# A hybrid attention and recurrence block: paired v products, the recurrence's products spread over four array tiles, and four changes of order

## The chip, the cores and the metric

The kernel is one program on one core of a Trainium2 chip. The core has five engines that work side by side, each through its own list of instructions in order: PE (the matrix engine, with its weight loads shown as PEld), DVE (the vector engine), ACT (the scalar engine), POOL and SP; SP and POOL mainly issue DMA transfers here. An instruction that needs a result of another engine waits at a semaphore, and all that stands behind it in its engine's list waits too. Results of PE land in PSUM, which is divided into banks of 128 partitions x 512 fp32 values; DVE and ACT read them from there ("evacuate" them) into SBUF.

The metric is the device time of one execution in microseconds (us). The kernel before takes 1640.1 us, the median of three runs that lie between 1639.86 and 1641.15 us.

## The reference

One block of a hybrid network works on 1024 positions of width 1024. Its input is normed and modulated, projected by one wide matrix, and goes through attention with a forget gate (8 heads) and through a recurrence (8 heads of width 64), whose outputs are gated, merged and projected; a feed-forward part with a convolution of width 3 follows.

```python
h = x
u = modulate(rms_norm(h, ln1_g), shift1, scale1)
q, k, v, f, p_rwkv, p_gate = split(u @ w_in)
o_fox = fox_attention(q, k, v, log_sigmoid(f + fox_b_f))
o_rwkv = rwkv7_time_mix(p_rwkv, ...)
merged = gate_fox * (o_fox @ fox_w_out) + gate_rwkv * (o_rwkv @ rwkv_w_out)
h = h + gate1 * (merged @ w_o)
h = h + gate2 * conv_ffn(modulate(rms_norm(h, ln2_g), shift2, scale2))
return rms_norm(h, final_g)

# the recurrence of one head inside rwkv7_time_mix, position by position
sa    = state @ a_t                                   # a_t = -kk
state = state * w_t + outer(sa, kk * a) + outer(v_t, k_t)
y_t   = state @ r_t
# then y is normed per head (mean, variance), a bonus is added, and it is multiplied by a gate
```

## The kernel before, in words

The part that matters here is the recurrence stage, from about 160 to 600 us of the span. It does three kinds of work at once, and a planner (`Weave`, in the code) interleaves them:

- **The recurrence in chunks.** The 8 heads are four head pairs p, and the 1024 positions two halves hf; that makes 8 units, k = 0 to 7 in the order (0,0), (0,1), (1,0) ... (3,1). A unit has 8 chunks of 64 positions. In place of a scan over positions, each chunk is solved with matrix products and one triangular inverse. `pre(k, p, hf)` prepares a unit (elementwise work, the products `p`, `q`, and the inverse), `main(k, p, hf)` finishes it.
- **Projections for attention and the recurrence**: `rkv_items` and `qk_steps` (products `ps_rkv`, `qk`), `gate_steps` (products `gt`).
- **The v projection of attention**, `v_steps`: 2 groups j of heads, each with 8 tiles t of 128 positions, 24 matmuls per tile (product `v`). ACT copies the result rounded (`vs`, L984) and DVE writes the remainder (`vs`, L985), and a DMA writes both to memory. Each tile has a PSUM tile of its own from the pool `big`, of which it uses 256 of 512 columns.

The order in which PE works is written by the planner and held as it is written. The order on the other engines is set by a scheduler when the kernel is built; it goes by its own estimates of when each operand is ready, and a few manual rules ("not before that one") bind it.

Inside a unit the steps are these. The matrices `E` are made from the products `p` (L794). The corner blocks of 32 x 32 of all chunks are inverted by 62 DVE steps, pairs of L814 (`t`) and L816 (`E`); their operands travel by DMA, `E` to `sm` to `M`, and the result by DMA, `E` to `se` to `TT`. Behind that `main` makes the other corners of the inverse: DVE transposes a corner (`X`, L872), PE makes the products `xi` and `zi`, ACT copies both out. Then the inverse products `uw`: for each of the 8 chunks and each of 2 heads one matmul of 64 rows by 64 columns with 128 values streamed, 16 in all. Chunks 0 to 3 go into one PSUM bank and 4 to 7 into another; head 0 uses rows and columns 0 to 63 of the array, head 1 uses 64 to 127. DVE copies one half of each result out (`Wt`, L900), ACT the other (`UV`, L902). The products `mz`, `sp`, `yp` and a chain of states `S` follow. At the end DVE subtracts the mean in `y` (L953): `mu` is the per-head mean of y, `va` that of its square, both made by `head_sums`, which also uses ACT (`Ztr`, `Zts`) and POOL (`Wtr`, `Wts`, L722).

Some further names: `QA` are operands of `uw`, copied by DVE at L841 and, from the product `q`, at L853; `ql` (L423) is the evacuation of a product `qk` on DVE; `k`, `v`, `r` of L397 are the evacuations of `ps_rkv`; `al` and `bk` at L772 to L774 are elementwise operands of `pre`.

Of the kernel before, what the change touches and what calls it, by code (L numbers as in the profile page):

```python
# [12 lines left out]
ALU = mybir.AluOpType  # L13
# [3 lines left out]
S = 1024  # L17
KT = 8
NH = 512
# [3 lines left out]
CH = 64  # L23
NCU = NH // CH
# [11 lines left out]
NOSYNC = mybir.DependencyInfo(mybir.DependencyClass.NoSync, mybir.DependencyReason.DATA)  # L36
# [98 lines left out]
def hybrid_block(ctx: ExitStack, tc: tile.TileContext, a, out):  # L135
    nc = tc.nc
    weave = Weave()
    ctx.enter_context(tc.manual_schedule(engines={mybir.EngineType.PE}))

    def mm(o, lhsT, rhs, start, stop, more=False):  # L140

        weave.mm_cost(o, lhsT, rhs)
        nc.tensor.matmul(o, lhsT, rhs, start=start, stop=stop, skip_group_check=more)  # L143
# [5 lines left out]
    def f32(ap):  # L149
        return ap.bitcast(F32)  # L150

    tt, stt, ts = nc.vector.tensor_tensor, nc.vector.scalar_tensor_tensor, nc.vector.tensor_scalar
# [15 lines left out]
    def V(name, i=0, n=1):  # L168
        o, _ = VEC[name]
        return vec[:, o + i : o + i + n]  # L170
# [78 lines left out]

    marks = {}  # L250
    held = []

    def behind(i, x):
        if x in marks:
# [119 lines left out]
    with ExitStack() as es:  # L374
# [4 lines left out]
        def big(name):  # L379
            return pb.tile([128, NH], F32, tag="big", name=name)  # L380

        def gen(name):
            return pr.tile([128, NH], F32, tag="gen", name=name)

        def shifted(w, ti, hf, dst, prev, name, by_kt=False):

            ps = big(f"ps_{name}{hf}")
            yield from gemm_steps(ps, w, u, slice(hf * NH, hf * NH + NH), by_kt=by_kt)
            sh = shp.tile([128, NH + 1], F32, tag="sh", name=f"sh_{name}{hf}")
            if hf == 0:  # L390
                nc.vector.memset(sh[:, 0:1], 0.0)
            else:
                nc.vector.tensor_copy(sh[:, 0:1], prev)
            nc.scalar.activation(sh[:, 1 : NH + 1], ps, AF.Copy, scale=V("mu", ti))
            if hf == 0:
                nc.gpsimd.tensor_copy(prev, sh[:, NH : NH + 1])
            marks["bank"] = stt(dst, ps, omu[:, ti : ti + 1], sh[:, 0:NH], op0=ALU.mult, op1=ALU.add)  # L397

        rkv, got, last_col = {}, {}, {}

# [13 lines left out]
        def qk_steps(w, i):  # L414
            sc_ = 0.125 if i < 4 else 1.0
            for hf in range(2):
                cs = slice(hf * NH, hf * NH + NH)
                ps = big(f"qk{i}_{hf}")
                yield from gemm_steps(ps, w, u, cs)
                hi = gsp.tile([128, NH], F32R, tag="sp0", name=f"qh{i}_{hf}")  # L420
                nc.scalar.activation(hi, ps, AF.Copy, scale=sc_)
                lo = gsp.tile([128, NH], F32R, tag="sp0", name=f"ql{i}_{hf}")
                stt(lo, ps, sc_, f32(hi), op0=ALU.mult, op1=ALU.subtract)  # L423
                h0 = 2 * (i % 4)
                for t, k, r0 in ((hi, 0, 0), (lo, 0, 64), (hi, 2, 0)) if i < 4 else ((hi, 1, 0), (hi, 1, 64), (lo, 3, 0)):
                    for h in range(2):
                        nc.sync.dma_start(f32(d_st[h0 + h, k, r0 : r0 + 64, cs]), f32(t[h * 64 : h * 64 + 64, :]))
# [274 lines left out]
        def c3(ap):  # L702
            return ap.rearrange("p (c s) -> p c s", s=CH)
# [23 lines left out]
        def pre(k, p, hf):  # L727
# [41 lines left out]
            tt(bk[:, :, 0, :], c3(kr), c3(en), op=ALU.mult)  # L769
            nc.gpsimd.tensor_copy(bk[64:128, :, 2, :], bk[64:128, :, 0, :])  # L770
            tt(ar[:, 1], c3(rr), el[:, :, 1:], op=ALU.mult)
            ts(al, al, V("k_a", p), oka[:, p : p + 1], op0=ALU.mult, op1=ALU.add)  # L772
            tt(al, al, kk, op=ALU.mult)
            tt(bk[:, :, 1, :], c3(al), c3(en), op=ALU.mult)  # L774
            pcd = chunk_tile("pcd", 3, NCU)
            nc.gpsimd.tensor_copy(pcd, el[:, :, CH])
            rkb = tmp("ksq")
# [33 lines left out]
            for s in range(31):  # L811
                J, W = s // 4 + 1, 31 - s
                tv = t32[:, 0 : J * W].rearrange("p (j w) -> p j w", w=W)
                tt(tv, E32[:, 0:J, s : s + 1].to_broadcast([128, J, W]),  # L814
                   M32[:, s : s + 1, s + 1 : 32].to_broadcast([128, J, W]), op=ALU.mult)
                tt(E32[:, 0:J, s + 1 : 32], E32[:, 0:J, s + 1 : 32], tv, op=ALU.add)  # L816
            se = scr.tile([2, NCU, 2, 32, 32], F32, tag="se", name=f"se{n}")
            for g in range(4):
# [31 lines left out]
            for c in range(NCU):  # L850
                for h in range(2):
                    mm(q[HS[h], c * CH : c * CH + CH], E[HS[1 - h], c, h, 0, :], UV[HS[1 - h], c, h, :], start=True, stop=True)
            nc.vector.tensor_copy(QA[:, :, 0, :], c3(q))  # L853
            bp = gen(f"bs{n}")
            yield from head_sums(bp, rkb, tmp("kr", dt=F32R), tmp("al", dt=F32R), True)
            bon = tmp("bon", bufs=2)
# [3 lines left out]
        def main(k, p, hf):  # L860
# [9 lines left out]
            yield max(0, o["ready"] - weave.now - 2500)  # L870
            for h in range(2):
                i = nc.vector.transpose(X[B0[h], :, :], TT[B0[h], :, 0:32])  # L872
                for x in ("S", "E", "bank") if k == 0 else ("S", "E", "QA") if k > 4 else ("S", "E"):
                    if x in marks:
                        tc.add_manual_dep(i.ins, marks[x].ins.name, NOSYNC)
            yield max(1300, o["ready"] - weave.now)
# [13 lines left out]

            yield 2000
            Wt = rw.tile([128, NCU, CH], F32, tag="Wt", name=f"Wt{n}", bufs=1)
            for c0 in range(0, NCU, 4):
                ps = gen(f"uw{n}{c0}")
                for c in range(c0, c0 + 4):
                    for h in range(2):
                        x = (c - c0) * 128
                        mm(ps[HS[h], x : x + 128], TT[HS[h], c, :], QA[HS[h], c, :, :], start=True, stop=True)
                pv = ps.rearrange("p (c a s) -> p c a s", a=2, s=CH)
                nc.vector.tensor_copy(Wt[:, c0 : c0 + 4, :], pv[:, :, 1, :])  # L900
                for h in range(2):
                    nc.scalar.copy(UV[HS[h], c0 : c0 + 4, h, :], pv[HS[h], :, 0, :])  # L902
            yield 2970
            Zt = rw.tile([128, NCU, CH], F32, tag="Zt", name=f"Zt{n}", bufs=1)
            for c0 in range(0, NCU, 4):
# [44 lines left out]
            mu = gen(f"mu{n}")  # L950
            yield 700
            yield from head_sums(mu, y, part("Zt", "r"), part("Wt", "r"))
            stt(y, mu, -1.0 / CH, y, op0=ALU.mult, op1=ALU.add)  # L953
            ysq = rw.tile([128, NH], F32, tag="ysq", name=f"ysq{n}", bufs=1)
            nc.scalar.activation(ysq, y, AF.Square)
            yield 2700
# [13 lines left out]
        def v_steps(w, j):  # L970

            for t in range(8):
                ts_ = slice(t * 128, t * 128 + 128)
                ps = big(f"v{j}_{t}")
                n = 0
                for wi, xi in ((0, 0), (0, 1), (1, 0)):
                    for kt in range(KT):
                        c0 = (kt % 4) * 256
                        mm(ps[:, 0:256], u[xi][:, kt, ts_], w[kt // 4][wi][:, c0 : c0 + 256], start=n == 0, stop=n == 23)
                        n += 1  # L980
                        yield
                vs = gsp.tile([128, 4, 2, 64], F32R, tag="sp0", name=f"vs{j}_{t}")
                pv = ps[:, 0:256].rearrange("p (h d) -> p h d", d=64)
                nc.scalar.copy(vs[:, :, 0, :], pv)  # L984
                tt(vs[:, :, 1, :], pv, f32(vs[:, :, 0, :]), op=ALU.subtract)  # L985
                nc.sync.dma_start(f32(d_v[4 * j : 4 * j + 4, :, t, :]).rearrange("h p x -> p h x"), f32(vs).rearrange("p h a d -> p h (a d)"))
# [1111 lines left out]
```

## Time and profile before

| | |
|---|---|
| median of 3 runs | 1640.1 us |
| profiled execution, its own time | 1639.56 us |
| its span (first to last instruction) | 1637.8 us |
| PE busy | 1600.6 us, 98% |
| DVE busy | 1214.5 us, 74% |
| ACT busy | 827.8 us, 51% |
| POOL busy | 157.4 us, 10% |
| mean granted clock of PE | 0.996 |

The profile shows one execution. Its chain of waits is the list of work that ended last, followed back from the end; shares are of the span. A group of rows gives engine, operation, tile and shape, with its count and the duration of one (minimum, median and maximum in ns, or the mean). In a timeline each row has its start (us from the start of the span), its length, engine, line, operation, output and input, shape and count, and in brackets the idle time of the engine just before it and who ended it. The ends of matmuls are modelled, so their rows overlap a little; their starts are measured.

### The profile page before, as it was taken

The numbers are of one execution on the slowest core, as the hardware profiler recorded it, in microseconds if no ns is written. First come the engines' busy times: TensorE is split into PE (matmuls) and PEld (weight loads), VectorE is DVE, ScalarE is ACT, GpSimd is POOL, SyncE is SP. The second block draws the span as 40 slices with busy tenths as digits, with TensorE's granted clock in tenths as the row PEclk, the third lists the DMA queues.
The fourth block names the chain that finished last, engine by engine and source line by source line (L and its number), as shares of the span: only waits on it lengthen the run. The fifth ranks groups of instructions, "written<-read, shape, count | busy, mean of one in ns | idle before, by whom it ended". The sixth has DMA issues, their size and how long they took to land.

```text
span 1637.8 us, 25963 instructions
## 1 busy us (share of the span) xinstructions
PE 1600.6 (98%) x9678; PEld 1334.4 (81%) x9678; DVE 1214.5 (74%) x2343; ACT 827.8 (51%) x1557; POOL 157.4 (10%) x189
## 2 busy tenths in 40 slices
PE   8999999999999999999999999999999999999998
PEld 7777787888978788888878888888888888888886
DVE  5786787878876536888679548987777777886677
ACT  5563344444455656778623225644444444555455
POOL 0011101111111011333122000000000000000000
PEclk9999999999999999999999999999999999999999
DMA  9496645543333336434197521232332332675363
GB/s 341 128 328 204 177 130 143 141 114 92 115 104 96 97 121 165 128 103 121 44 357 264 187 81 39 71 135 97 114 105 97 101 105 96 232 249 161 122 212 109
DMA packets 123542, 238.79 MB, mean 146 GB/s; under 512 B 42188, under 2 KB 51284, under 8 KB 123416
## 3 DMA queue, kind: packets, MB, share of 16 engines
q1 hardware_dynamic: 114936, 218.77, 41.2%
q0 software_dynamic: 8480, 18.37, 4.2%
q8 instruction: 76, 1.25, 0.3%
q14 instruction: 50, 0.41, 0.1%
HBM read 172.57 MB, written 64.50 MB: 145 GB/s over the span
## 4 chain that ended last, share of the span: by engine, by line
PE 71%; DVE 6%; ACT 2%; issue 1%; DMA 1%; SPq 1%; POOL 0%; DVEq 0%; POOLq 0%; ACTq 0%
PE X L143 15%; PE D L143 13%; PE Y L143 7%; PE gt L143 6%; PE wo L143 5%; PE br L143 4%; PE rk_ps L143 4%; PE W L143 4%; PE ps_rkv L143 3%; PE ov L143 2%; PE lg L143 2%; PE tp L147 1%; PE v L143 1%; PE sp L143 1%; DVE quads L1082 1%
## 5 line engine op out<-in xcount | busy, mean ns | idle before, releaser
L143 PE MATMUL D<-op,op 128*128 128x512 f32 x924 | 209.8, 389 | 0.0
L143 PEld LDWEIGHTS D<-op,op 128*128 128x128 f32 x924 | 173.3, 188 | 36.3 <-DVE op L1302 0.3
L143 PE MATMUL X<-T_m,S 128*128 128x512 f32 x440 | 107.1, 390 | 0.0
L143 PEld LDWEIGHTS X<-T_m,S 128*128 128x128 f32 x440 | 82.4, 188 | 17.8 <-ACT T_m L1781 0.5
L1301 ACT CAST op<-g 128x512 fp32r<-128x512 f32 x77 | 47.8, 621 | 73.0 <-PE D L143 48.2
L1302 DVE TENSOR_TENSOR op<-g,op 128x512 fp32r<-128x512 f32 x77 | 53.0, 689 | 40.8 <-ACT op L1301 40.8
L1560 DVE SCALAR_TENSOR_TENSOR c<-ab,vec,c 128x512 f32<-128x512 f32 x88 | 65.8, 750 | 18.4 <-ACT c L1563 16.8
L814 DVE TENSOR_TENSOR t<-E,M 128x60 f32<-128x60 f32 (+24 forms) x248 | 56.4, 227 | 27.5 <-DMA M<-sm 21.5
L1526 DVE TENSOR_TENSOR A<-ur,A 128x512 fp32r<-128x512 f32 x64 | 44.0, 689 | 38.3 <-ACT A L1522 38.2
L1526 DVE TENSOR_TENSOR S<-ur,S 128x512 fp32r<-128x512 f32 x66 | 45.5, 691 | 35.2 <-ACT S L1522 35.1
L1522 ACT CAST S<-ur 128x512 fp32r<-128x512 f32 x66 | 41.0, 622 | 57.3 <-DVE ur L1515 30.3
L298 DVE TENSOR_TENSOR lo_in<-raw_in,hi_in 128x512 fp32r<-128x512 f32 x84 | 57.6, 726 | 15.8 <-PE gt L143 4.8
L143 PE MATMUL Y<-T_h,A 128*128 128x512 f32 x264 | 63.4, 389 | 0.0
L143 PE MATMUL Y<-T_h,S 128*128 128x512 f32 x264 | 63.3, 389 | 0.0
L1122 DVE TENSOR_TENSOR tl<-tp,th 128x512 fp32r<-128x512 f32 (+1 forms) x80 | 50.0, 631 | 15.3 <-ACT th L1119 14.9
L1522 ACT CAST A<-ur 128x512 fp32r<-128x512 f32 x64 | 39.6, 621 | 42.9 <-PE X L143 33.4
L296 ACT CAST hi_in<-raw_in 128x1024 fp32r<-128x1024 f32 x42 | 43.8, 1048 | 34.2 <-PE qk L143 14.0
L816 DVE TENSOR_TENSOR E<-E,t 128x60 f32<-128x60 f32 (+24 forms) x248 | 56.0, 226 | 6.3
L143 PE MATMUL W<-B_f,A 128*128 128x512 f32 x252 | 60.6, 389 | 0.0
L143 PE MATMUL X<-B_b,A 128*128 128x512 f32 x252 | 60.5, 389 | 0.0
L143 PEld LDWEIGHTS Y<-T_h,S 128*128 128x128 f32 x264 | 49.6, 188 | 10.3
L143 PEld LDWEIGHTS Y<-T_h,A 128*128 128x128 f32 x264 | 49.5, 188 | 10.3
(491 smaller groups left out, 4143.1 us busy)
## 6 DMA issues: line engine op xcount, KB each, us to landing
raw_in<-in_w_in SPq DMA_DIRECT2D x50, 512.0 KB
wm<-in_w_mod SPq DMA_DIRECT2D x48, 512.0 KB
ur<-in_w_up SPq DMA_DIRECT2D x44, 512.0 KB
g<-d_g SPq DMA_DIRECT2D x35, 512.0 KB
d_g<-gs SPq DMA_DIRECT2D x44, 256.0 KB
d_g<-c SPq DMA_DIRECT2D x33, 256.0 KB
d_st<-qh SPq DMA_DIRECT2D x64, 128.0 KB
stA<-d_st POOLq DMA_DIRECT2D x8, 1024.0 KB, 7.3
```

What stands on the lines that cost most here:

```text
L143: nc.tensor.matmul(o, lhsT, rhs, start=start, stop=stop, skip_group_check=more)
L147: nc.tensor.transpose(o, i, eye)
L296: nc.scalar.copy(hi, raw)
L298: nc.vector.tensor_tensor(lo[:, c : c + NH], raw[:, c : c + NH], f32(hi[:, c : c + NH]), op=ALU.subtract)
L814: tt(tv, E32[:, 0:J, s : s + 1].to_broadcast([128, J, W]), M32[:, s : s + 1, s + 1 : 32].to_broadcast([128, J, W]), op=ALU.mult)
L816: tt(E32[:, 0:J, s + 1 : 32], E32[:, 0:J, s + 1 : 32], tv, op=ALU.add)
L1122: tt(tl[:, 0:w], tp[:, 0:w], f32(th[:, 0:w]), op=ALU.subtract)
L1301: nc.scalar.copy(hi, src)
L1302: tt(lo, src, f32(hi), op=ALU.subtract)
L1522: nc.scalar.copy(hi, src)
L1526: tt(lo, src, f32(hi), op=ALU.subtract)
L1560: stt(c, ab[:, x + hf * NH : x + hf * NH + NH], V("conv_w", 22 * x + i), c, op0=ALU.mult, op1=ALU.add)
```

## The change

It has five parts.

1. **Paired v products.** A tile `v` of odd t no longer takes a PSUM tile of its own. It writes columns 256 to 511 of the bank in whose columns 0 to 255 the even tile before it stands.
2. **Steps behind read-outs.** The three `al` operations of a unit (L772 to L774) are remembered, and if an evacuation on DVE (L397 or L423) is written within 3000 ns of the planner's time after them, they are bound to come behind it on DVE (`evac_done`).
3. **The first step behind the copy.** The first step of the first unit's inverse is bound to come behind the copy of `q` into `QA` (`after_this`).
4. **The odd chunks' products in the other half.** In `uw`, even chunks keep their places in the array and go to one bank; odd chunks take the other half of the columns (head 0 rows 0 to 63 and columns 64 to 127, head 1 the reverse) and go to a second bank. The two kinds alternate. The copies `Wt` become one of 128 x 256 and two of 64 x 256 instead of two of 128 x 256; those of `UV` stay four.
5. **Transpositions behind y.** For k above 4, the transposes `X` (L872) are bound to come behind the last `y` (L953).

```diff
+    soft = []
+    def evac_done(i):
+        for x, t in soft:
+            if weave.now - t < 3000:
+                tc.add_manual_dep(x.ins, i.ins.name, NOSYNC)
+        soft.clear()
+        return i
+    first_step = []
+    def after_this(i):
+        for x in first_step:
+            tc.add_manual_dep(x.ins, i.ins.name, NOSYNC)
...
-            marks["bank"] = stt(dst, ps, omu[:, ti : ti + 1], sh[:, 0:NH], op0=ALU.mult, op1=ALU.add)
+            marks["bank"] = evac_done(stt(dst, ps, omu[:, ti : ti + 1], sh[:, 0:NH], op0=ALU.mult, op1=ALU.add))
...
-                stt(lo, ps, sc_, f32(hi), op0=ALU.mult, op1=ALU.subtract)
+                evac_done(stt(lo, ps, sc_, f32(hi), op0=ALU.mult, op1=ALU.subtract))
...
-            ts(al, al, V("k_a", p), oka[:, p : p + 1], op0=ALU.mult, op1=ALU.add)
-            tt(al, al, kk, op=ALU.mult)
-            tt(bk[:, :, 1, :], c3(al), c3(en), op=ALU.mult)
+            soft.clear()
+            soft.append((ts(al, al, V("k_a", p), oka[:, p : p + 1], op0=ALU.mult, op1=ALU.add), weave.now))
+            soft.append((tt(al, al, kk, op=ALU.mult), weave.now))
+            soft.append((tt(bk[:, :, 1, :], c3(al), c3(en), op=ALU.mult), weave.now))
...
+                if k == 0 and s == 0:
+                    first_step.append(i)
...
-            nc.vector.tensor_copy(QA[:, :, 0, :], c3(q))
+            after_this(nc.vector.tensor_copy(QA[:, :, 0, :], c3(q)))
+            first_step.clear()
...
-                for x in ("S", "E", "bank") if k == 0 else ("S", "E", "QA") if k > 4 else ("S", "E"):
+                for x in ("S", "E", "bank") if k == 0 else ("S", "E", "QA", "y") if k > 4 else ("S", "E"):
...
-            for c0 in range(0, NCU, 4):
-                ps = gen(f"uw{n}{c0}")
-                for c in range(c0, c0 + 4):
-                    for h in range(2):
-                        x = (c - c0) * 128
-                        mm(ps[HS[h], x : x + 128], TT[HS[h], c, :], QA[HS[h], c, :, :], start=True, stop=True)
-                pv = ps.rearrange("p (c a s) -> p c a s", a=2, s=CH)
-                nc.vector.tensor_copy(Wt[:, c0 : c0 + 4, :], pv[:, :, 1, :])
+            ps = [gen(f"uw{n}{e}") for e in range(2)]
+            for c in range(NCU):
                 for h in range(2):
-                    nc.scalar.copy(UV[HS[h], c0 : c0 + 4, h, :], pv[HS[h], :, 0, :])
+                    x = c // 2 * 128
+                    mm(ps[c % 2][HS[h ^ c % 2], x : x + 128], TT[HS[h], c, :], QA[HS[h], c, :, :], start=True, stop=True)
+            pv = [x.rearrange("p (c a s) -> p c a s", a=2, s=CH) for x in ps]
+            nc.vector.tensor_copy(Wt[:, 0::2, :], pv[0][:, :, 1, :])
+            for h in range(2):
+                nc.vector.tensor_copy(Wt[HS[h], 1::2, :], pv[1][HS[1 - h], :, 1, :])
+            for e in range(2):
+                for h in range(2):
+                    nc.scalar.copy(UV[HS[h], e::2, h, :], pv[e][HS[h ^ e], :, 0, :])
...
-            stt(y, mu, -1.0 / CH, y, op0=ALU.mult, op1=ALU.add)
+            marks["y"] = stt(y, mu, -1.0 / CH, y, op0=ALU.mult, op1=ALU.add)
...
-                ps = big(f"v{j}_{t}")
+                if t % 2 == 0:
+                    pair = big(f"v{j}_{t}")
+                ps = pair[:, t % 2 * 256 : t % 2 * 256 + 256]
...
-                        mm(ps[:, 0:256], u[xi][:, kt, ts_], w[kt // 4][wi][:, c0 : c0 + 256], start=n == 0, stop=n == 23)
+                        mm(ps, u[xi][:, kt, ts_], w[kt // 4][wi][:, c0 : c0 + 256], start=n == 0, stop=n == 23)
...
-                pv = ps[:, 0:256].rearrange("p (h d) -> p h d", d=64)
+                pv = ps.rearrange("p (h d) -> p h d", d=64)
```

What this does to the engines' lists shows at three places. On PE the sequence of work is the same in both, apart from the inner order of `uw`. The first place is PE where tile 5 of the second group of v products begins (`v1_4` is tile 4 of group 1; `hi_v`, `lo_v` are the two parts of the weights, and "waits DVE" means a wait at DVE's semaphore). Before:

```order
L143 MATMUL v1_4_4900<-lo_v10_4418,u_hi_107 128x256 x4
L143 MATMUL v1_4_4900<-lo_v11_4425,u_hi_107 128x256 x4
L143 MATMUL v1_5_5001<-hi_v10_4417,u_hi_107 128x256 [waits DVE_49]
L143 MATMUL v1_5_5001<-hi_v10_4417,u_hi_107 128x256 x3
L143 MATMUL v1_5_5001<-hi_v11_4424,u_hi_107 128x256 x4
```

and with the change, on the same engine at the same place:

```order
L143 MATMUL v1_4_4899<-lo_v10_4418,u_hi_107 128x256 x4
L143 MATMUL v1_4_4899<-lo_v11_4425,u_hi_107 128x256 x4
L143 MATMUL v1_4_4899<-hi_v10_4417,u_hi_107 128x256 [waits DVE_49]
L143 MATMUL v1_4_4899<-hi_v10_4417,u_hi_107 128x256 x3
L143 MATMUL v1_4_4899<-hi_v11_4424,u_hi_107 128x256 x4
```

Both begin the new tile with a wait for DVE. Before, the value waited for was that of the remainder `vs` of the tile two before (`v1_3`), whose PSUM tile `v1_5` takes over; now it is that of the tile just before, `v1_4`, because both lie in one bank and the framework counts a bank as one object. The same holds for all eight odd tiles.

The second place is DVE around the remainder of that tile 4. Before, the steps of the inverse stand at a width of 14 there (the last number of `128x5x14`; it falls by one with each pair of steps):

```order
L814 TENSOR_TENSOR t322_1_4562<-E322_1_4560,M322_1_4555 128x70
L773 TENSOR_TENSOR al3_0_4808<-al3_0_4808,k30_4094 128x512
L816 TENSOR_TENSOR E322_1_4560<-E322_1_4560,t322_1_4562 128x5x14
L985 TENSOR_TENSOR vs1_4_4997<-v1_4_4900,vs1_4_4997 128x4x64
L774 TENSOR_TENSOR bk3_0_4888<-al3_0_4808,en3_0_4815 128x8x64
L778 SCALAR_TENSOR_TENSOR ksq3_0_4973<-r30_4093,vec_72,al3_0_4808 128x512
L814 TENSOR_TENSOR t322_1_4562<-E322_1_4560,M322_1_4555 128x65
```

and with the change:

```order
L828 TENSOR_TENSOR t322_1_4562<-E322_1_4560,M322_1_4555 128x42
L787 TENSOR_TENSOR al3_0_4807<-al3_0_4807,k30_4093 128x512
L832 TENSOR_TENSOR E322_1_4560<-E322_1_4560,t322_1_4562 128x7x6
L1006 TENSOR_TENSOR vs1_4_4996<-v1_4_4899,vs1_4_4996 128x4x64
L788 TENSOR_TENSOR bk3_0_4887<-al3_0_4807,en3_0_4814 128x8x64
L792 SCALAR_TENSOR_TENSOR ksq3_0_4972<-r30_4092,vec_72,al3_0_4807 128x512
L828 TENSOR_TENSOR t322_1_4562<-E322_1_4560,M322_1_4555 128x35
```

The remainder stands between the same neighbours, but the inverse has gone on from a width of 14 to one of 6: eight pairs of steps, 16 instructions, stand ahead of it now that stood behind it. The remainder of tile 2 of the same group comes 7 steps later in the same way, and that of tile 4 of the first group 5 steps later.

The third place is DVE where `y` of unit 4 (`y2_0`) meets the transposes `X2_1` of unit 5. Before:

```order
L841 COPY QA3_0_5099<-at3_0_5270 64x4x64 x4
L872 STREAM_TRANSPOSE X2_1_5383<-TT2_1_4630 32x256
L953 SCALAR_TENSOR_TENSOR y2_0_5152<-mu2_0_5154,y2_0_5152 128x512
L872 STREAM_TRANSPOSE X2_1_5383<-TT2_1_4630 32x256
L853 COPY QA3_0_5099<-q3_0_5320 128x8x64
L814 TENSOR_TENSOR t323_0_5194<-E323_0_5192,M323_0_5187 128x31
```

and with the change:

```order
L857 COPY QA3_0_5096<-at3_0_5267 64x4x64 x4
L972 SCALAR_TENSOR_TENSOR y2_0_5149<-mu2_0_5151,y2_0_5149 128x512
L889 STREAM_TRANSPOSE X2_1_5380<-TT2_1_4630 32x256 x2
L828 TENSOR_TENSOR t323_0_5191<-E323_0_5189,M323_0_5184 128x31
L832 TENSOR_TENSOR E323_0_5189<-E323_0_5189,t323_0_5191 128x31
```

The subtraction now stands ahead of both transposes. In SP's list at that point, the DMAs `se2_1` and `TT2_1`, which feed these transposes, move ahead of the last writes of `vs`; before they stood behind them, and `TT2_1` in the middle of the four DMAs `sm3_0` that feed the next unit's inverse.

More of the change, by code (lines that the diff above doesn't have):

```diff
@@ L813, in pre @@
                 tv = t32[:, 0 : J * W].rearrange("p (j w) -> p j w", w=W)
-                tt(tv, E32[:, 0:J, s : s + 1].to_broadcast([128, J, W]),
-                   M32[:, s : s + 1, s + 1 : 32].to_broadcast([128, J, W]), op=ALU.mult)
+                i = tt(tv, E32[:, 0:J, s : s + 1].to_broadcast([128, J, W]),
+                       M32[:, s : s + 1, s + 1 : 32].to_broadcast([128, J, W]), op=ALU.mult)
+                if k == 0 and s == 0:
+                    first_step.append(i)
                 tt(E32[:, 0:J, s + 1 : 32], E32[:, 0:J, s + 1 : 32], tv, op=ALU.add)
```

## The prediction

> **What bounds the kernel now.** I read the page's busy times first, then the chain of waits by engine, then the clock.
>
> ```profile
> PE 1600.6 (98%) x9678; PEld 1334.4 (81%) x9678; DVE 1214.5 (74%) x2343; ACT 827.8 (51%) x1557; POOL 157.4 (10%) x189
> PE 71%; DVE 6%; ACT 2%; issue 1%; DMA 1%; SPq 1%; POOL 0%; DVEq 0%; POOLq 0%; ACTq 0%
> core 0: 1637.8 us, clock 0.996
> ```
>
> The reader sees one engine that is busy for 98% of the span and granted its full clock. So time falls only where PE's own work shrinks or where it stands still, and every new wait of PE costs its length. The waits of PE between 160 and 610 us, the recurrence stage, are few (total us, times, longest):
>
> ```profile
> PE qk L143 <- DVE ql L423: 2.3, 1, 2.3
> PE ps_rkv L143 <- DVE k L397: 1.4, 1, 1.4
> PE v L143 <- DVE vs L985: 1.3, 2, 0.8
> PE sp L143 <- ACT S L933: 0.9, 1, 0.9
> PE va L143 <- POOL Wts L722: 0.9, 1, 0.9
> PE mu L143 <- POOL Wtr L722: 0.7, 1, 0.7
> PE va L143 <- ACT Zts L719: 0.6, 1, 0.6
> PE zi L143 <- ACT X L882: 0.6, 1, 0.6
> ```
>
> They add to 8.7 us: that is all that moving steps can win here. Two stretches matter for what follows, since the v products lie in them (length; busy us and instructions of PE, PEld, DVE, ACT, POOL; PE's clock; DMA share; GB/s):
>
> ```profile
> 314.20:346.00 31.80, 31.33 (x373) 29.03 (x370) 30.15 (x96) 13.23 (x29) 4.51 (x8) 1.00 0.34 106
> 417.50:446.00 28.50, 27.72 (x336) 26.21 (x335) 26.60 (x87) 10.55 (x24) 2.07 (x6) 1.00 0.29 85
> ```
>
> DVE is busy for 95% and 93% there. A result that PE wants from DVE comes late in these stretches, whenever PE asks.
>
> **Part 1, paired v products.** The work stays the same; what changes is which remainder `vs` an odd tile waits for. In the rows of before, each odd tile's start on PE and the remainder of the even tile just ahead stand as follows, tiles 1, 5, 7 of the first group and 1, 3, 5, 7 of the second:
>
> ```profile
> 323.03 0.77 PE L143 MATMUL v<-hi_v,u_hi 128*128 128x256 f32 x5
> 324.46 0.42 DVE L985 TENSOR_TENSOR vs<-v,vs 128x256 fp32r<-128x256 f32 x1
> 342.85 0.86 PE L143 MATMUL v<-hi_v,u_hi 128*128 128x256 f32 x5 [0.47 <-DVE vs L985]
> 343.79 0.42 DVE L985 TENSOR_TENSOR vs<-v,vs 128x256 fp32r<-128x256 f32 x1
> 351.09 0.28 PE L143 MATMUL v<-hi_v,u_hi 128*128 128x256 f32 x1
> 351.70 0.42 DVE L985 TENSOR_TENSOR vs<-v,vs 128x256 fp32r<-128x256 f32 x1
> 411.83 0.40 PE L143 MATMUL v<-hi_v,u_hi 128*128 128x256 f32 x2
> 413.62 0.42 DVE L985 TENSOR_TENSOR vs<-v,vs 128x256 fp32r<-128x256 f32 x1
> 421.83 0.40 PE L143 MATMUL v<-hi_v,u_hi 128*128 128x256 f32 x2
> 424.00 0.42 DVE L985 TENSOR_TENSOR vs<-v,vs 128x256 fp32r<-128x256 f32 x1
> 434.20 0.52 PE L143 MATMUL v<-hi_v,u_hi 128*128 128x256 f32 x3
> 437.78 0.42 DVE L985 TENSOR_TENSOR vs<-v,vs 128x256 fp32r<-128x256 f32 x1
> 441.68 0.40 PE L143 MATMUL v<-hi_v,u_hi 128*128 128x256 f32 x2
> 442.76 0.42 DVE L985 TENSOR_TENSOR vs<-v,vs 128x256 fp32r<-128x256 f32 x1
> ```
>
> The wait now needed is the remainder's start plus 0.42 less PE's start: 1.85, 1.36, 1.03, 2.21, 2.59, 4.00 and 1.50 us, 14.5 us in all. Tile 3 of the first group has other work of PE between it and tile 2, and costs nothing. PE's list keeps its order, so nothing can be done in these waits: behind the waiting matmul stand the rest of the tile, then the recurrence's products.
>
> The sum of lags isn't yet the answer, for two reasons. While PE waits, DVE works on at its own pace, so inside one dense stretch the later lags contain the earlier waits. And the order on DVE moves: the remainders of tile 4 (first group), tile 2 and tile 4 (second group) come 5, 7 and 16 steps later. A step costs what this group says (busy us, mean ns of one, then idle before):
>
> ```profile
> L814 DVE TENSOR_TENSOR t<-E,M 128x60 f32<-128x60 f32 (+24 forms) x248 | 56.4, 227 | 27.5 <-DMA M<-sm 21.5
> ```
>
> 5, 7 and 16 times 0.227 are 1.1, 1.6 and 3.6 us. First stretch: PE is 1.85 late after tile 1, and 1.36 + 1.1 = 2.5 late after tile 5 (the larger, not the sum); tile 7 lies behind the stretch and adds its 1.0: 3.5 us. Second stretch: 2.2 after tile 1, 2.6 + 1.6 = 4.2 after tile 3, 4.0 + 3.6 + 0.4 = 8.0 after tile 5 (the 0.4 is one more copy `Wt`, part 4); there the old wait of tile 6 for that same remainder, 0.8, falls away, and tile 7 adds 1.5: 8.7 us. Part 1 costs **12.2 us**. Its bounds: the shortest lag of a row, 1.03, seven times is 7.2 (DVE free whenever asked); all lags and all moves added up is 14.5 + 6.3 = 20.8.
>
> **Part 4, `uw` over four tiles of the array.** In the chain of waits, the first and last of four units in which PE paces itself (us, length):
>
> ```profile
> 374.75 1.89 PE uw L143 x32
> 570.24 1.89 PE uw L143 x32
> L143 PE MATMUL uw<-QA,TT x256: 269/269/320, 230.3 to 571.9; 64*64 64x128 f32 x128
> 465.29 0.69 PE L143 MATMUL xi<-X,E 32*32 32x32 f32 x32
> L900 DVE COPY Wt<-uw x16: 415/418/425, 234.0 to 572.2; 128x256 f32<-128x256 f32 x16
> ```
>
> 32 records in 1.89 us, of which the last takes 0.27, start (1.89 - 0.27)/31 = 52 ns apart, though each lasts 269: two halves of the array overlap already. The `xi` row has starts 16 ns apart with shorter operands, so issuing isn't the limit. If four quarters overlap as well as two, a unit's starts need half of 1.7 us and it saves 0.85; if not, nothing. No row shows four quarters at once. I take 0.85, because the overlap that the rows do show is one without loss. Only four units (1_1, 2_1, 3_0, 3_1) lie where PE isn't soon stopped by DVE or POOL; in the others PE arrives earlier at a wait that doesn't move. That is **-3.4 us**, between 0 and -6.8 (all eight). The price is one more copy on DVE per unit, at most 0.42 us, hidden where DVE has slack and counted above where it hasn't. The four `UV` copies on ACT, busy half of the time, stay four.
>
> The Trainium skill, "TensorEngine Tiling (Array Packing)", section "Available Configurations" and "Key Properties", lists 64 x 64 as four tiles that run independently; by it the saving is the 0.85 I take, and the sum without that would stand 3.4 us higher. This case's trace shows only two of them at work.
>
> **Parts 2 and 3, the first copy and the steps behind read-outs.**
>
> ```profile
> 179.77 0.19 DVE L814 TENSOR_TENSOR t<-E,M 128x31 f32<-128x31 f32 x1 [7.01 <-DMA M<-sm]
> 180.11 0.68 DVE L853 COPY QA<-q 128x512 f32<-128x512 f32 x1
> ```
>
> DVE sat idle for 7 us while the 0.68 us copy stood behind a step that waited for a DMA. Now it runs in that hole, and `ql`, for which PE waits 2.3 us, comes 0.7 to 1.0 earlier; `k`, for which it waits 1.4, gets `al` (0.5) out of its way. I take -1.4 together and give 0.3 back at the wait of `mu` for POOL, which keeps its own pace: **-1.1 us**, between 0 and -3.7 (both waits gone).
>
> **Part 5, transpositions behind y.**
>
> ```profile
> 458.40 0.43 DVE L872 STREAM_TRANSPOSE X<-TT 32x256 f32<-32x256 f32 x1 [3.23 <-DMA TT<-se]
> 458.86 0.69 DVE L953 SCALAR_TENSOR_TENSOR y<-mu,y 128x512 f32<-128x512 f32 x1
> 461.56 2.77 DMA M<-sm
> ```
>
> DVE stood 3.23 us at a transpose whose operand was on its way, with `y` behind it, and the waits of `va` (0.9 and 0.6) and of `zi` (0.6) follow. With `y` ahead, and `TT` asked for earlier on SP, all three should go: **-2.1 us**, between 0 and -2.1. What can be late next is the transpose; its operand's DMAs stand ahead of the last writes of `vs` now, so I see no cost.
>
> **The sum.** 12.2 - 3.4 - 1.1 - 2.1 = +5.6 us. Behind the recurrence PE is again the bound, and the shift stays whole. The profiled execution took 1639.56 us and becomes 1645.2; the median of the runs lies 0.5 above it, so I predict 1645.7 us. 0.2% (3.3 us) is about what a measurement of this kernel can tell from no change.
>
> **Rivals.**
>
> - *Faster.* The lags shrink to the least one, because PE arrives later and DVE has caught up: 7.2 us. All eight `uw` gain (-6.8), and the waits for `ql`, `k`, `va` and `zi` go (-5.8). -5.4 us, 1634.7. It decides once the lags together cost less than about 8 us. For it: each wait gives DVE time. Against it: the order on DVE puts more steps ahead of the remainders, in stretches where DVE is busy 93 to 95%.
> - *Hardly any change.* The lags cost 8 to 9 us and the other three parts win 6 to 9: within 3 us of now.
> - *Four quarters don't overlap.* Then -3.4 goes: +9.0, 1649.1. For it: no row shows four; against: two do overlap cleanly.
> - *The clock.* In the two stretches the granted clock was 1.00, and the longest wait above is 2.3 us. Tile 5 of the second group now stands about 4 us. If a wait of that length halves the clock for as long again, 4 us of work take 6 to 8: +2 to +4 on top, 1648 to 1650. The Trainium skill, "TensorE: Matmul & The Clock Gate", section "HAM oscillation — how this bites in real kernels", has such a rule, with idle gaps above about 3.4 us as its limit. No run here shows it in the recurrence, so the sum leaves it out.
>
> **How the numbers follow.** The forecast gets 0.50 (its own range 1642 to 1650: waits 9 to 16 us); quarters that don't overlap 0.12, and the clock 0.08, both slower; hardly any change 0.16; faster 0.14. So slower has 0.70, the same 0.16, faster 0.14. The range 1638 to 1654 leaves out most of the faster case (1 in 10) and the end where all lags and moves add up (less than 1 in 10).
>
> **What would show it.** In the waits of PE, `v` for `vs` should grow from 1.3 us to about 12, with a longest of 3 to 5 us at tile 5 of the second group; the waits of `va` and `zi` should be gone, and that of `ql` near 1.3. A unit's `uw` should last about 1.05 us in the chain; 1.89 would say that the quarters don't overlap. If the waits for `vs` come to less than 8 us, the forecast is wrong in its main term: then DVE wasn't as tightly bound to its order as I read it. Wrong too if a wait appears at `sp` or `mz` for the new copies `Wt`, or if the granted clock falls after 435 us.

## The result, and the profile after

The changed kernel takes 1654.9 us, the median of five runs (1652.3 to 1656.4), against 1640.1 us before: a ratio of 1.0089 with a 95% interval of 1.0077 to 1.0100. It is slower by 0.9%, 14.8 us. The profiled execution took 1654.58 us, with a span of 1652.8 us. Its page has this line of busy times, and its view of cores this one:

```profile
PE 1601.0 (97%) x9678; PEld 1332.7 (81%) x9678; DVE 1218.5 (74%) x2351; ACT 827.5 (50%) x1557; POOL 155.4 (9%) x189
```

```profile
core 0: 1652.8 us, clock 0.993
```

PE runs the same 9678 matmuls and is busy for as long as before, 1601 us, in a longer span, and the granted clock has gone from 0.996 to 0.993. The waits of PE between 160 and 625 us (total us, times, longest) show the first half of the answer:

```profile
PE v L143 <- DVE vs L1006: 14.0, 7, 3.3
PE qk L143 <- DVE ql L436: 1.6, 1, 1.6
PE p L143 <- DVE bk L788: 1.0, 1, 1.0
PE sp L143 <- ACT S L952: 0.9, 1, 0.9
PE mu L143 <- POOL Wtr L735: 0.8, 1, 0.8
PE ps_rkv L143 <- DVE k L410: 0.5, 1, 0.5
PE mz L143 <- DVE Wt L916: 0.5, 1, 0.5
PE q L143 <- ACT UV L921: 0.5, 1, 0.5
PE mz L143 <- DVE t L828: 0.4, 1, 0.4
PE mz L143 <- DVE Wt L918: 0.3, 2, 0.2
```

The wait of `v` for `vs` has grown from 1.3 us in two places to 14.0 us in seven; the waits of `va` and `zi` are gone, those of `ql` and `k` shorter, and `mz`, `q` and `p` have waits that weren't there. The second half stands in the windows view. Each row is one stretch of 3.41 us; the fixed grid on which such stretches lie is worked out in the last section. Three groups of neighbours are shown (length; busy us and instructions of PE, PEld, DVE, ACT, POOL; PE's granted clock; DMA share; GB/s):

```profile
321.81:325.23 3.42, 1.68 (x14) 1.35 (x12) 3.42 (x9) 0.37 (x1) 0.00 (x0) 1.00 0.48 153
325.23:328.64 3.41, 3.41 (x43) 3.35 (x43) 3.19 (x11) 1.88 (x4) 0.19 (x1) 0.50 0.48 159
...
342.29:345.70 3.41, 2.16 (x19) 1.96 (x17) 3.31 (x10) 0.69 (x2) 0.36 (x1) 1.00 0.00 0
345.70:349.12 3.42, 2.25 (x19) 2.25 (x20) 1.61 (x9) 0.32 (x1) 0.00 (x0) 1.00 0.57 163
349.12:352.53 3.41, 3.41 (x32) 3.41 (x30) 0.42 (x1) 1.00 (x3) 0.00 (x0) 1.00 0.21 34
...
448.11:451.52 3.41, 1.05 (x8) 1.05 (x9) 3.38 (x8) 0.00 (x0) 0.77 (x1) 1.00 0.04 12
451.52:454.93 3.41, 3.41 (x18) 3.41 (x17) 1.89 (x11) 0.08 (x1) 0.00 (x0) 0.50 0.23 65
```

Each row with a clock of 0.50 stands behind a row in which PE was busy for half of the time or less. There are four such slow stretches in the recurrence, at 325, 421, 434 and 452 us, each 3.41 us long, and PE was busy for 1.68, 1.31, 0.87 and 1.05 us in the stretches ahead of them. PE was busy all through the slow ones, so each cost half of its length, 1.7 us. The kernel before has none there. The waits ahead of them are those of odd v tiles; these are two of them, and between them a wait that no slow stretch follows:

```profile
324.44 0.85 PE L143 MATMUL v<-hi_v,u_hi 128*128 128x256 f32 x5 [1.74 <-DVE vs L1006]
346.87 0.39 PE L143 MATMUL v<-hi_v,u_hi 128*128 128x256 f32 x1 [2.42 <-DVE vs L1006]
450.47 0.74 PE L143 MATMUL v<-hi_v,u_hi 128*128 128x256 f32 x4 [3.29 <-DVE vs L1006]
```

The first wait, of 1.74 us, lies inside one stretch of the grid and is followed by half clock; the second is longer, 2.42 us, but a boundary of the grid (345.70) cuts it in two, and nothing follows.

Since PE's list is the same in both kernels apart from the inner order of `uw`, the time from each PE instruction's start to the next can be compared one by one. Summed by place, the difference of the two spans (15.0 us) is made of:

| | us |
|---|---|
| waits of `v` for `vs` | +13.5 |
| four stretches at half clock, 1.7 us each | +6.8 |
| `uw` itself, eight units (-6.1, and 0.8 of the line above lies in one of them) | -6.9 |
| `mz` behind the copies `Wt` +4.0, `p` behind `bk` +1.0, `q` behind `UV` +0.5 | +5.5 |
| waits of `va` and `zi` gone | -2.8 |
| waits of `ql` and `k` shorter | -1.5 |
| small differences that I didn't follow | +0.4 |

The four quarters of the array do overlap. This is the first unit's `uw` on PE's timeline, before and after:

```profile
230.34 1.96 PE L143 MATMUL uw<-QA,TT 64*64 64x128 f32 x32
229.55 1.10 PE L143 MATMUL uw<-QA,TT 64*64 64x128 f32 x32
```

In the chain of waits a unit that took 1.89 us takes 1.03. This is what came behind it in the changed kernel, on DVE:

```profile
234.13 0.42 DVE L916 COPY Wt<-uw 128x256 f32<-128x256 f32 x1
234.71 0.87 DVE L918 COPY Wt<-uw 64x256 f32<-64x256 f32 x2
```

and on PE:

```profile
234.60 0.44 PE L143 MATMUL mz<-E,Wt 64*64 64x128 f32 x4 [0.51 <-DVE Wt L916]
235.19 0.99 PE L143 MATMUL mz<-E,Wt 64*64 64x128 f32 x8 [0.16 <-DVE Wt L918]
```

`mz` takes the chunks in order, so its second chunk, an odd one, needs the copies of 64 partitions, which come last on DVE: its first odd matmuls start at 235.19 and 235.64 us, just behind the ends of the two copies at 235.14 and 235.59. Before, its first four chunks needed the first copy alone. Most of this delay lies inside `mz`, where the view of waits hardly shows it, since the modelled ends of the matmuls cover it; the starts show 4.0 us of it over five units.

### The profile page after: what moved, and what is told of

It reads as the page before. It is cut to its first block, busy times and chain, and to the rows that moved or that the text cites. A ratio compares the mean times of both kernels' runs of the same rounds, so it can differ in the third digit from the quotient of the medians.

```text
span 1652.8 us, 25967 instructions
## 1 busy us (share of the span) xinstructions
PE 1601.0 (97%) x9678; PEld 1332.7 (81%) x9678; DVE 1218.5 (74%) x2351; ACT 827.5 (50%) x1557; POOL 155.4 (9%) x189
## 4 chain that ended last, share of the span: by engine, by line
PE 69%; DVE 8%; ACT 2%; DMA 2%; issue 1%; SPq 0%; POOL 0%; DVEq 0%; ACTq 0%; POOLq 0%
PE X L143 15%; PE D L143 13%; PE Y L143 7%; PE wo L143 5%; PE gt L143 5%; PE br L143 4%; PE rk_ps L143 4%; PE W L143 4%; PE ps_rkv L143 3%; PE ov L143 2%; PE lg L143 2%; PE v L143 1%; PE tp L147 1%; DVE E L832 1%; DVE t L828 1%
```

## The experiments

Theory A: the loss is the waits of the odd tiles for their neighbour's remainder, and the slow clock that these waits set off; the other parts together save a little. Theory B: the loss lies in the moved steps and additional copies on DVE, and `v` only shows it. Twelve kernels were run. Each was compared with runs of the kernel before on the same chip.

**Part 1 taken back.**

```diff
-                if t % 2 == 0:
-                    pair = big(f"v{j}_{t}")
-                ps = pair[:, t % 2 * 256 : t % 2 * 256 + 256]
+                ps = big(f"v{j}_{t}")
...
```

> The changed kernel with part 1 taken back (each v tile in a PSUM tile of its own), the other four parts kept. Theory A, the loss is the waits of the odd tiles and the slow clock that they set off: 1654.9 less 13.5 us of waits and less 6.8 us (four stretches at half clock, 1.7 us each), about 1635 us, with no stretch of half clock in the recurrence and waits of v for vs back near 1 us. Theory B, the loss comes from the moved steps and the additional copies on DVE, and the waits of v only show it: above 1643 us.

Measured: 1639.4 us, ratio 1.0007 (0.9998 to 1.0015) to the kernel before. Theory B is out, since 0.8 of the 0.9% went with the pairs. Theory A is right about the pairs but not about the rest, which was to gain 4 us and gained nothing. Of the 6.9 us that `uw` saves, `mz` behind the copies `Wt` takes 3.4 by the starts. The waits of `v` (total, times, longest) and two neighbouring stretches of the windows view show where most of the rest went; the waits:

```profile
PE v L143 <- DVE vs L1004: 3.3, 2, 1.7
```

and the stretches:

```profile
339.63:343.04 3.41, 1.79 (x15) 1.59 (x14) 3.21 (x12) 0.69 (x2) 0.00 (x0) 1.00 0.19 53
343.04:346.45 3.41, 3.41 (x19) 3.41 (x18) 1.82 (x10) 0.31 (x1) 0.00 (x0) 0.50 0.39 106
```

PE, faster by `uw`, arrives earlier at two remainders on the busy DVE and waits 1.6 and 1.7 us there. Both waits fall inside one stretch of the grid, and each is followed by 3.41 us at half clock (343 and 439 us), 3.4 us lost in all.

**Part 1 alone.**

```diff
-                ps = big(f"v{j}_{t}")
+                if t % 2 == 0:
+                    pair = big(f"v{j}_{t}")
+                ps = pair[:, t % 2 * 256 : t % 2 * 256 + 256]
...
```

> The kernel before with part 1 alone. Theory A: 1640.1 plus some 13 us of waits plus 3 to 7 us for two to four stretches at half clock, 1656 to 1661 us, waits of v for vs of 12 to 15 us in seven places. Theory B: below 1645 us.

Measured: 1655.7 us, just under the range of theory A, ratio 1.0102 (1.0088 to 1.0117). The waits of `v` for `vs` are 16.2 us in seven places, the longest 4.9, and four stretches ran at half clock behind them. Part 1 alone is the whole loss, as theory A has it. By the starts of PE's instructions the waits of `v` cost 15.8 us and the clock 5.7 (less than four times 1.7, since PE stood idle for 2.2 us of one of the four); that 16 us remain of 21.5 is because the waits of `va` and `ql` shrank by 3.6 us, as `y` and `ql` had time to come, and the part ahead of 150 us was 1.9 us shorter in this execution.

**PE kept busy in the waits.** Dummy products fill the waits; the real products overwrite what they write, and they are additional work.

```diff
...
+                if t % 2 == 1 and FILL[j][t // 2]:
+                    if t < 7:
+                        ahead = big(f"v{j}_{t + 1}")
+                        spare = ahead
+                    for x in range(FILL[j][t // 2]):
+                        nc.tensor.matmul(spare[:, 0:256], u[0][:, x % 8, ts_], w[0][0][:, 0:256], start=True, stop=True)
```

> The changed kernel with dummy products of PE ahead of five odd tiles' waits (14, 19, 16, 20 and 26 matmuls of 0.117 us, written into the next pair's bank, where the real products overwrite them): PE arrives at the same wait, busy instead of idle. Theory A1, idle time of PE sets off the slow clock: no stretch of half clock is left in the recurrence, 1654.9 less 6.8, about 1648 us. Theory A2, the slow stretches come from something else (the mix of products, DVE's traffic): they stay, 1653 to 1657 us.

Measured: 1649.7 us, ratio 1.0068 (1.0056 to 1.0080). Not one stretch between 150 and 640 us is below full clock, and little of the waits is left. The waits (the second row is a dummy's):

```profile
PE v L143 <- DVE vs L1015: 3.6, 5, 1.0
PE v L1004 <- DVE vs L1015: 1.0, 1, 1.0
```

and in the windows view:

```profile
300.00:450.00 150.00, 145.21 (x1595) 127.44 (x1595) 120.98 (x345) 65.40 (x131) 24.34 (x35) 1.00 0.37 106
450.00:640.00 190.00, 184.93 (x1567) 151.08 (x1566) 107.21 (x266) 106.13 (x198) 23.91 (x25) 1.00 0.41 116
```

The span is 4.9 us below that of the changed kernel, although, by the starts of PE's instructions, the waits of `v` with the dummies in them take 2.6 us longer than the waits alone did. So 7.5 us came back elsewhere: 6.8 is what the four slow stretches cost, and 0.7 is left for small differences elsewhere. The time, 1649.7 us, is nearer to A1's 1648 than to A2's range. A2 is out: with the same waits, but PE busy in them, no half clock follows.

**Part 4 alone.**

```diff
-            for c0 in range(0, NCU, 4):
-                ps = gen(f"uw{n}{c0}")
+            ps = [gen(f"uw{n}{e}") for e in range(2)]
...
+                    mm(ps[c % 2][HS[h ^ c % 2], x : x + 128], TT[HS[h], c, :], QA[HS[h], c, :, :], start=True, stop=True)
...
```

> The kernel before with part 4 alone (the products uw over four quarters of the array, one more copy Wt per unit). If the copies are hidden as I costed them: 6.1 us less for uw, some of it lost at waits of DVE and POOL, 1635 to 1637 us. If the copies Wt delay mz as the changed kernel's trace shows (1.9 us at mz, 0.5 at q): 1637 to 1639 us. If DVE's work is the bound there, nothing is gained: 1640 us.

Measured: 1640.5 us, ratio 1.0011 (1.0002 to 1.0021): the worst of the cases expected, though `uw` itself gained its 6.9 us. In the profiled execution 2.0 us of it went to waits of `v` for `vs`, 3.8 to `mz` and `q`, and 3.4 to the clock, behind the waits of `va` that the kernel before has too; shorter waits of `ql` and `zi` gave some of it back. The stretches at `va`:

```profile
461.73:465.14 3.41, 1.69 (x7) 1.09 (x7) 0.11 (x1) 2.69 (x5) 1.27 (x1) 1.00 0.55 160
465.14:471.96 6.82, 6.82 (x47) 5.05 (x46) 6.14 (x24) 4.63 (x8) 0.00 (x0) 0.50 0.32 114
```

**Parts 2, 3 and 5 alone.** The edit is the diff of these parts.

> The kernel before with parts 2, 3 and 5 alone (the changes of order). From the changed kernel's trace: ql 0.7 to 1.5 us, k 0.7 us, va 1.9 us and zi 0.6 us less waiting, p up to 1.0 us more if the transposes behind y delay bk: 1636 to 1638 us. If part 5's gain hung on TT being asked for earlier on SP, as it was with pairs: the waits come back as others and it is 1639 to 1640 us.

Measured: 1638.3 us, ratio 1.0000 (0.9991 to 1.0009), between the two cases. The trace shows the second: the waits of `va` and `zi` went, but `ps_rkv` waits 1.4 us for `gs`, with one stretch at half clock behind it (464 us, 1.7 us lost), and `p` 1.0 us for `bk` in their place. With the pairs, SP asks for `TT` ahead of the DMAs `sm`; here, as in the kernel before, `TT` stands among them. That part 5's gain hangs on this order was not tried alone.

**Pairs two apart.**

```diff
...
+                if t % 4 < 2:
+                    pairs[t % 2] = big(f"v{j}_{t}")
+                ps = pairs[t % 2][:, t % 4 // 2 * 256 : t % 4 // 2 * 256 + 256]
```

> The changed kernel with the same half banks, but tiles t and t + 2 share a bank in place of t and t + 1, so that an odd tile waits for the remainder of the tile two before, as in the kernel before. Theory A, it is the wait for the neighbour: as with part 1 taken back, 1638 to 1641 us, waits of v for vs about 3 us. Theory C, writing into the second half of a bank that is being read costs PE time by itself: over 1645 us.

Measured: 1640.3 us, ratio 1.0008 (1.0000 to 1.0017), with waits of `v` for `vs` of 3.3 us and two steps at half clock (466 us), here behind a wait for `gs`. Time and waits are as with part 1 taken back. Half a bank costs nothing by itself that these runs can tell; the wait for the neighbour does.

**The remainders ahead.** From here on I looked for what keeps the other parts from gaining. The first edit binds five or six operations of `pre` behind the two remainders that PE waited for, and lets `mz` go by even and odd chunks. In this kernel and all that follow, each v tile has a PSUM tile of its own again, and part 5 binds the transposes of unit 5 alone:

```diff
...
+    def vs_ahead(j, t, i):
+        k, xs = {(0, 3): (4, (2, 4, 5, 6, 7)), (1, 4): (6, (1, 2, 4, 5, 6, 7))}.get((j, t), (None, ()))
+        for x in xs:
+            tc.add_manual_dep(pre_ops[k][x].ins, i.ins.name, NOSYNC)
...
-            for c0 in range(0, NCU, 4):
-                ps = gen(f"mz{n}{c0}")
-                for c in range(c0, c0 + 4):
+            for e in range(2):
+                ps = gen(f"mz{n}{e}")
+                for c in range(e, NCU, 2):
...
```

> Part 1 taken back; parts 2 to 4 kept; part 5 for k = 5 alone; and two things added: mz, Zt and Mt go by even and odd chunks, so that mz can begin with the first copy Wt, and the remainders vs of tile 3 of the first group and of tile 4 of the second come ahead of the operations of pre (kr, bk, al, ksq) that they stood behind. Theory A with the clock as I now read it (a window of 3.41 us with PE idle for half of it or more is followed by one at half clock): both waits of v of 1.6 us go and with them two slow windows of 1.7 us each, mz gains 1 us: 1639.4 less 3.3, less 3.4, less 1: 1632 to 1635 us. If other waits take their place: 1637 to 1640 us.

Measured: 1639.2 us, ratio 0.9999 (0.9990 to 1.0007). The waits of `v` fell to 1.5 us and no slow stretch follows them, but `ps_rkv` now waits 2.4 us for `gs`, and 10.24 us at half clock follow that. So it is the second case expected.

The same with the old `uw` and `mz`:

> The kernel before with parts 2 and 3, part 5 for k = 5 alone, and the two remainders vs ahead of the operations of pre; uw and mz stay as in the kernel before. From the waits: v 1.3 less, ql and k 2 less, va and zi 0 to 2 less: 1635 to 1638 us. Against the kernel before it tells what the order alone is worth, against the other one with the remainders ahead what uw over four quarters is worth when DVE isn't in its way (up to 6 us).

Measured: 1637.5 us, ratio 0.9990 (0.9982 to 0.9999), with the wait for `gs` again, 2.6 us, and 6.83 us at half clock behind it. The timelines show its cause, on DVE:

```profile
457.84 0.69 DVE L878 COPY QA<-q 128x512 f32<-128x512 f32 x1
462.32 0.19 DVE L837 TENSOR_TENSOR t<-E,M 128x31 f32<-128x31 f32 x1 [3.79 <-DMA M<-sm]
463.55 0.68 DVE L387 SCALAR_TENSOR_TENSOR gs<-gt,gs 128x512 f32<-128x512 f32 x1
```

and on PE:

```profile
464.29 2.14 PE L143 MATMUL ps_rkv<-u_hi,hi_in 128*128 128x512 f32 x6 [2.61 <-DVE gs L387]
```

DVE stands idle for 3.79 us at a step that waits for a DMA; `gs`, whose operand ACT had finished at 456.8 by its own timeline, stands six instructions behind it.

**The gate's evacuation first.** The first step of that inverse (unit 6) is bound behind `gs`, with `uw` over four quarters and with the old one:

```diff
...
+            if (i, hf) == (0, 0) and 6 in step0:
+                tc.add_manual_dep(step0[6].ins, gs_mark[0, 0].ins.name, NOSYNC)
...
```

> As the kernel with the remainders ahead (uw over four quarters, mz by even and odd chunks), and the first step of unit 6's inverse is bound behind the evacuation gs of the first gate product, which stood behind six steps that waited for a DMA (PE waited 2.4 us, and three windows at half clock followed). If that wait sets the clock off: 1639.2 less 2.4 and less up to 5.1: 1632 to 1634 us, no slow window between 150 and 640 us. If another wait takes its place at xi or zi: 1636 to 1640 us.

> The same binding in the kernel with the remainders ahead and the old uw (PE waited 2.6 us there, two windows at half clock followed): 1637.5 less 2.6 and less 3.4: 1631 to 1634 us if the clock stays up. Beside the one with uw over four quarters it tells what that part is worth without waits and slow windows: 0 to 5 us.

Measured: 1640.9 us, ratio 1.0009 (0.9999 to 1.0018), and 1637.3 us, ratio 0.9989 (0.9980 to 0.9997). Both lie above what was expected. The wait of `ps_rkv` for `gs` went in both, and another took its place at `va`, 2.5 us. In the first kernel it lies inside one stretch of the grid (PE idle for 2.36 us there) and 10.24 us at half clock follow it; in the second a boundary of the grid cuts it (1.04 and 1.45 us idle in the two stretches) and none follow. In the second, the timelines show the cause of the wait, a copy of `bk` ahead of `Wts` on POOL:

```profile
501.34 3.18 POOL L793 COPY bk<-bk 64x512 f32<-64x512 f32 x1 [6.00 <-DVE bk L792]
504.60 1.60 POOL L744 TENSOR_TENSOR Wts<-ysq,Zts 128x512 fp32r<-128x512 f32 x1
```

and on PE:

```profile
506.25 0.50 PE L143 MATMUL va<-Wts,blk_r 128*128 128x512 f32 x1 [2.49 <-POOL Wts L744]
```

**That copy on ACT.**

```diff
-            nc.gpsimd.tensor_copy(bk[64:128, :, 2, :], bk[64:128, :, 0, :])
+            (nc.scalar.copy if k == 7 else nc.gpsimd.tensor_copy)(bk[64:128, :, 2, :], bk[64:128, :, 0, :])
```

> The kernel with the first gate product's evacuation first and the old uw, and the copy of bk for unit 7 goes to ACT: on POOL it stood ahead of Wts, for which PE waited 2.5 us at va. 1637.3 less 2.5: 1634 to 1636 us, no wait of PE over 1.5 us between 150 and 625 us, no slow window there.

> The same with uw over four quarters and mz by even and odd chunks. PE saves 6.9 us in uw; if the waits at mz, mu, k and v that grew with it (4 to 5 us) and a slow window or two (1.7 us each) eat it: 1636 to 1640 us, no better than with the old uw; if it is kept: below 1633 us.

Measured with the old `uw`: 1635.1 us, ratio 0.9979 (0.9971 to 0.9988). This kernel is as fast as expected, and faster than both, by 0.2% than the kernel before and, by the two ratios, by 1.1% than the changed one. Its waits between 150 and 625 us:

```profile
PE va L143 <- POOL Wts L744: 1.5, 1, 1.5
PE rk_ps L143 <- ACT gm L1236: 1.2, 1, 1.2
PE mu L143 <- POOL Wtr L744: 0.8, 1, 0.8
PE sp L143 <- ACT S L965: 0.8, 1, 0.8
PE qk L143 <- DVE ql L445: 0.7, 1, 0.7
PE ps_rkv L143 <- DVE k L419: 0.6, 1, 0.6
```

and in the windows view:

```profile
150.00:450.00 300.00, 297.74 (x2844) 252.71 (x2843) 245.59 (x688) 133.28 (x256) 46.21 (x66) 1.00 0.49 135
450.00:640.00 190.00, 186.14 (x1514) 152.32 (x1513) 109.67 (x273) 111.27 (x211) 23.52 (x25) 1.00 0.40 114
```

Measured with `uw` over four quarters: 1637.9 us, ratio 0.9995 (0.9986 to 1.0004). `uw` is again 6.9 us shorter, and the kernel 2.8 us longer: PE waits 2.4 us at `mz` for `Wt` and 1.7 at `v` for `vs`, 1.4 us more at `mu` and `sp` together, and one slow stretch at 474 us costs 1.7. So part 4 is worth nothing here either, as expected: the two largest of these waits are for DVE, which has one more copy per unit. That this copy alone is the reason was not tried.

## Why the prediction was wrong

The direction was right and its main mechanism too; the time lies 0.9 us above the range, and the predicted loss of 5.6 us was 14.8. Two of the signs that were named for a wrong forecast came: a wait of `mz` for the copies `Wt`, and a clock that falls after 435 us.

- **The clock** is the step that failed. It stood as a rival of 0.08, "so the sum leaves it out", since the longest wait before, 2.3 us, showed a clock of 1.00, and only a wait of about 4 us was thought to set it off, for 2 to 4 us. Measured, four waits of 1.74 to 3.29 us did, and cost 6.8 us, shown by the stretches and by the dummies that took them away. The reading of before was at fault: its 2.3 us proves nothing about other waits of that length, since what counts is how a wait lies in the grid, and a boundary at 186.58 cut this one in two: PE was idle for 1.4 and 0.9 us of the two stretches (the rows of before below). The Trainium skill, "TensorE: Matmul & The Clock Gate", section "What's actually happening", says that the hardware watches a free-running activity window of about 3.4 us; the trace agrees, in stretches of 3.41 us. The section "HAM oscillation — how this bites in real kernels" of that page of the Trainium skill, from which I took that only gaps above 3.4 us matter, doesn't agree: 1.74 us was enough, and here the measurement decides.

```profile
187.48 0.73 PE L143 MATMUL qk<-u_hi,hi_in 128*128 128x512 f32 x2 [2.26 <-DVE ql L423]
```

```profile
183.17:186.58 3.41, 2.05 (x9) 1.33 (x8) 3.34 (x9) 1.02 (x2) 0.33 (x1) 1.00 0.56 129
186.58:190.00 3.42, 2.52 (x11) 2.08 (x12) 3.18 (x12) 1.82 (x4) 0.30 (x1) 1.00 0.45 87
```

- **Part 1** was sized well: 12.2 us predicted, 13.5 measured (8.7 and 8.6 in the second stretch, 3.5 and 5.0 in the first, where tile 5 waited 1.9 more, not 0.65). Its longest wait stands at tile 5 of the second group, as said.
- **Part 4**: the quarters do overlap, but all eight units gained, -6.9 in place of -3.4. Against that, the copy that I costed at nothing outside the dense stretches delayed `mz` by 4.0 us, and `q` came 0.5 later. Net it is -2.4, and near the -3.4 by luck, since two errors cancel in the main.
- **Parts 2 and 3**: -1.5 for -1.1. **Part 5**: -2.8 for -2.1 in the changed kernel, where I saw no cost, but `p` waits 1.0 us for `bk` behind the transposes. In the two runs without pairs, parts 2, 3 and 5 alone and part 1 taken back, a wait of `ps_rkv` for `gs` of 1.4 us takes most of that gain, so it isn't one that part 5 brings by itself.

Without the clock the measured time would have been 1648.1 us (1654.9 less 6.8), inside the range, against 1645.7 predicted. That neither part 4 nor part 5 gains once the pairs are gone is not what I would have said.

## What to carry to other kernels

Where the framework counts a bank as one object, as here, a tile that takes the other half of a bank waits for the last reader of the first half: place it two tiles on, not next, if PE shall not stand. Price a wait of a matrix engine that is otherwise busy not by its length alone: if, in a trace like these, it can fill about half of one stretch of 3.4 us, add 1.7 us or more for the stretches that follow at half clock. When PE gets faster in a stage where other engines deliver, look first for what stands in their lists behind an instruction that waits, since that is where the gain went here.

## What the runs showed of the hardware that I had not expected

- The granted clock changes on a fixed grid of 3.413 us: every slow stretch in these traces (before the last one at a kernel's end) is one, two or three times that long, and the four in the changed kernel start a whole number of steps apart (325.23, 420.80, 434.45, 451.52).
- What counts, in steps at full clock, is PE's idle time within one step of that grid. Over the profiles of the two kernels and the twelve experiments, between 150 and 640 us: all 13 steps at full clock with 1.72 us idle or more (51%) were followed by half clock, none of those with 1.37 us or less, and four of the ten between 1.40 and 1.69 us. So the bound lies near half, and something beside the idle time, whose ends are modelled, decides near it; what, stays open. Of the 24 steps that ran at half clock themselves, eight were followed by another one: in one of these PE stood idle for 2.2 us, in the other seven only for 0.0 to 0.9 us. So idle time isn't all that decides when the clock comes back, and what else does stays open too.
- The grid lies differently in each execution (in twelve of the fourteen profiles the first slow stretch of the span begins somewhere between 41.4 and 44.1 us). That would let the same wait cost 1.7 us in one execution and nothing in the next, and so spread the runs of one kernel over several us, as 1637.8 to 1644.8 us with part 1 taken back. That the spread comes from this was not tested, but the clocks of the executions go with it: in the 123 executions of the twelve experiments a longer span than the kernel's mean mostly has a lower granted clock (correlation -0.6); with part 1 taken back, the longest has 0.992 and the five shortest 0.996 to 0.998.
